# Block 2's attention with plain float32 products of 64 rows or columns, two heads at a time

## Chip, cores and metric

One core of a Trainium2 chip runs the whole program in one launch. The metric is the device time of the execution in microseconds. The engines are the tensor engine (PE, with its weight loads as PEld), the vector engine (DVE), the scalar engine (ACT), GpSimd (POOL) and the sync engine (SP), which issues the DMAs of the weights.

## The reference, cut

A first block (a mixer with pooling, attention and a recurrent branch, then a gated feed-forward layer), and after it a block of two layers, whose mixer has three kinds of attention with heads of 64 channels. Sequence 256, model width 2048, all float32.

```python
# layer l of block 2
h = rmsnorm_2(x, norm_mix[l])
qa, ka, va, qb, kb, vb, qc, kc, vc = jnp.split(h @ w_in[l], IN_SPLITS, axis=-1)
oa = window_attention(qa, ka, va, a_sink[l], t5_table)   # 8 heads, 2 of keys and values; bias, sink
ob = neighborhood_attention(qb, kb, vb, b_rpb[l])        # 8 heads; bias and a mask by column
oc = axial_global_attention(qc, kc, vc, c_q_gain[l], c_k_gain[l])  # 16 heads, 4 of keys; rms norm, rotary
# each: s = q k.T / 8 (+ bias); p = softmax(s); o = p v
mix = concat([rmsnorm_2(oa, ...), rmsnorm_2(ob, ...), rmsnorm_2(oc, ...)])
x = x + mix @ w_o[l]
u = relu(rmsnorm_2(x, norm_mlp[l]) @ w_up[l])
x = x + (u * u) @ w_down[l]
```

## The kernel before

Everything large is a product of activations (features on the partitions, 256 tokens in the free dimension) with a weight that is streamed from HBM in units of 128 x 1024 values. A unit is loaded by SP into one of 7 buffers, cut into a high and a low part of type float32r (line 136 on ACT, line 137 on DVE; 3 buffers each), and used in three float32r products per piece (lines 332 to 334, or 347 to 349 where the tokens are the output's partitions). `drive` writes the order by hand: the split of the next unit, then the products of this one, then one `step`.

The rest of the work runs beside the products as Python generators: each `step` advances every active generator by one stage and lets queues start new ones. The queue "rope" holds the norm and rotary part of C's keys and queries (lines 1459 to 1499, from line 1467 on ACT, a product with a block matrix on line 1470, and so on through DVE, ACT and POOL), the queue "head" the attention heads, one started per 1.4 steps. The order of instructions on each engine is that of the program; PE executes attention products between those of the units. Four PSUM banks ("a") are handed round among all generators, oldest first.

One head of block 2 (`head`, from line 1560) before the change: for each pair of heads `queries` (lines 1456 and 1457) makes [high; low] of one head's 64 query channels and [low; high] in 128 partitions; keys (`kk`) lie as high parts in both halves of the partitions and low parts in both, so that two products of 128 rows add all four combinations:

```python
nc.tensor.matmul(sc[:, i, :], qs[:, t], kh, start=True, stop=False)
nc.tensor.matmul(sc[:, i, :], qs[:, t], kl, start=False, stop=True)
```

This is done for two blocks of 128 queries: four float32r products. `softmax` (lines 1049 to 1067) takes the row maximum on DVE, the exponential on ACT, and scales; four transposes (line 1073) turn p; its high part is written on ACT (line 357), its low part on DVE (line 362); v has its high part in the first 64 output columns and its low part in the last 64, so four products (line 1620) give both halves, which line 1625 (ACT copies the lower half) and line 1626 (DVE adds it to the upper one) put together and write to `L["q"]`. Keys of A and C are split when they are made; B's keys for each pair of heads, in front of its scores. After the heads of a kind, `norm` (line 419 for the diagonal, 424 for the broadcast) prepares the rows for w_o.

Block 1's attention (`fox`) uses plain float32 products of full size, lines 1089, 1092 and 1108.

Of the kernel before, what the change touches and what calls it, by code (L numbers as in the profile page):

```python
# [9 lines left out]
F32 = mybir.dt.float32  # L10
F32R = mybir.dt.float32r
# [46 lines left out]
def shape_constants():  # L58
    """Arrays that follow from the shapes alone."""
# [59 lines left out]
class Unit:  # L119
    """A [128, nk, ncols] piece of a weight: loaded, cut into two float32r parts, used on the tensor engine."""  # L120
# [24 lines left out]
class Ada:  # L145
    """128 rows x 1024 columns of w_ada times silu(c), summed over the row tiles on the vector engine."""
# [44 lines left out]
def weave(a, b):  # L191
    """the two lists, evenly interleaved"""
# [7 lines left out]
class Builder:  # L200
# [51 lines left out]
    def bank(self):  # L252
        """the same for a PSUM bank"""
# [23 lines left out]
    def more_groups(self):  # L277
        """two of the banks go over to the column groups"""
# [3 lines left out]
    def fewer_groups(self):  # L282
        """the column groups leave them again; put back once what is in them has been read"""
# [37 lines left out]
    def mm_b(self, u, ps, X, first, last, k0=None, ncols=None):  # L321
        """PSUM[nb] += W[:, nb].T X for the rows of one unit; X = (hi, lo), features on the partitions."""
# [13 lines left out]
    def mm_a(self, u, outs, X, first, last, c0, n, shared=False):  # L336
        """outs[half] += X[:, half].T W for the rows of one unit: tokens on the partitions."""
# [13 lines left out]
    def split_to(self, hi, lo, src, scale=1.0):  # L351
        """hi + lo = src * scale, both float32r."""
# [36 lines left out]
    def sumsq_add(self, acc, src, first, scale=1.0):  # L389
        """acc (+)= (src * scale)^2"""  # L390
# [8 lines left out]
    def tok_sums(self, ps, *tiles):  # L399
        """Sum over the partitions of tiles of [128, n x 256] -> PSUM [128 tokens, 2]."""  # L400
# [9 lines left out]
    def rstd_of(self, r, ss, n):  # L410
        """r = (ss / n + eps) ** -0.5 of [128, 2]"""
# [9 lines left out]
    def bcast(self, ps, r, dg):  # L421
        """r [128 tokens, 2] -> PSUM [128, 256], each token's value in all partitions."""
# [1513 lines left out]
```

## Time and profile before

| | us |
|---|---|
| time, median of 3 runs | 3420.06 |
| lowest and highest | 3419.43 and 3421.57 |
| span of the profiled execution (its own time is not given apart) | 3419.7 |
| PE busy, PEld busy | 3282.7, 3231.9 |
| DVE busy, ACT busy, POOL busy | 2213.9, 1629.8, 294.4 |

Times in the profile are counted from the start of the span. Matmuls are pipelined: the record of one lasts longer than the distance to the next, so sums over records are more than the engine's time, and distances between starts are to be used. A plain float32 matmul leaves two records.

### The profile page before, as it was taken

The page shows a single profiled execution, that of the slowest core. Times are in us where ns is not written, and L with a number is a line of the kernel's source. Part 1 is how long each engine was busy: PE and PEld are TensorE (multiplying, and loading weights), DVE is VectorE, ACT ScalarE, POOL GpSimd, SP SyncE. Part 2 cuts the span into 40 slices and gives each one's busy share as a digit, 9 for nine tenths or more (in the row PEclk, how much of TensorE's full clock was granted, in tenths as well). Part 3 has the DMA queues.
Part 4 walks back from the last instruction along what each step waited for, and adds up shares of the span by engine and source line. Part 5 has one row for each costly group of instructions (what it writes and reads, how often), then busy time and mean ns, then how long its engine had stood idle before and what let it go on. Part 6 is the DMA issues. An engine that isn't in the chain of part 4 may idle for free.

```text
span 3419.7 us, 64015 instructions
## 1 busy us (share of the span) xinstructions
PE 3282.7 (96%) x26612; PEld 3231.9 (95%) x26612; DVE 2213.9 (65%) x2921; ACT 1629.8 (48%) x2236; POOL 294.4 (9%) x250
## 2 busy tenths in 40 slices
PE   7989899979999998999999999999999999999998
PEld 7988889979999998989999999998889999999998
DVE  7898887537745668976545454556897655545454
ACT  4436345424434456865434343445775533334344
POOL 0021100000000032111000000012110100000000
PEclk9999999999999999999999999999999999999999
DMA  9986896659866554545666665665454656666563
GB/s 360 336 286 224 300 318 225 187 169 304 273 200 187 184 160 122 162 143 180 185 185 185 185 186 183 186 182 154 133 161 153 182 184 185 185 185 185 183 186 125
DMA packets 390722, 683.96 MB, mean 200 GB/s; under 512 B 40823, under 2 KB 97952, under 8 KB 390176
## 3 DMA queue, kind: packets, MB, share of 16 engines
q1 hardware_dynamic: 390144, 679.56, 62.8%
q8 instruction: 208, 3.41, 0.4%
q14 instruction: 82, 0.67, 0.1%
q10 hardware_dynamic: 288, 0.31, 0.0%
HBM read 677.62 MB, written 8.46 MB: 201 GB/s over the span
## 4 chain that ended last, share of the span: by engine, by line
PE 77%; DVE 6%; DMA 2%; issue 2%; ACT 2%; SPq 1%; POOL 0%; ACTq 0%; DVEq 0%; POOLq 0%
PE pg L334 24%; PE pg L332 24%; PE pg L333 24%; DVE wlo L137 2%; ACT whi L136 1%; DMA raw<-in_w_ffn_up 1%; DMA raw<-in_w_ffn_gate 1%; DMA raw<-in_w_out 1%; PE pa L1620 1%; PE pa L1073 1%; DVE qs L1457 1%; DVE kB L362 0%; PE pa L1556 0%; DVE pr L1049 0%; DVE ada L171 0%
## 5 line engine op out<-in xcount | busy, mean ns | idle before, releaser
L137 DVE TENSOR_TENSOR wlo<-raw,whi 128x1024 fp32r<-128x1024 f32 x1064 | 1319.0, 1241 | 1089.0 <-ACT whi L136 1084.9
L136 ACT ACTIVATE whi<-raw 128x1024 fp32r<-128x1024 f32 x1064 | 1123.4, 1058 | 1554.0 <-PE pg L333 1254.1
L332 PE MATMUL pg<-xh,whi 128*128 128x256 f32 x5184 | 1478.6, 285 | 24.6 <-ACT whi L136 20.0
L334 PE MATMUL pg<-xh,wlo 128*128 128x256 f32 x5184 | 1468.2, 283 | 16.3 <-DVE wlo L137 16.2
L333 PE MATMUL pg<-xl,whi 128*128 128x256 f32 x5184 | 1467.0, 283 | 1.8 <-DVE xl L565 1.1
L332 PEld LDWEIGHTS pg<-xh,whi 128*128 128x128 f32 x5184 | 988.3, 191 | 30.4 <-ACT whi L136 21.2
L334 PEld LDWEIGHTS pg<-xh,wlo 128*128 128x128 f32 x5184 | 987.0, 190 | 20.8 <-DVE wlo L137 20.4
L333 PEld LDWEIGHTS pg<-xl,whi 128*128 128x128 f32 x5184 | 987.7, 191 | 6.9 <-issue 2.7
L332 PE MATMUL pg<-u,whi 128*128 128x256 f32 x2048 | 579.9, 283 | 0.0
L333 PE MATMUL pg<-u,whi 128*128 128x256 f32 x2048 | 579.5, 283 | 0.0
L334 PE MATMUL pg<-u,wlo 128*128 128x256 f32 x2048 | 579.5, 283 | 0.0
L333 PEld LDWEIGHTS pg<-u,whi 128*128 128x128 f32 x2048 | 393.1, 192 | 0.0
L334 PEld LDWEIGHTS pg<-u,wlo 128*128 128x128 f32 x2048 | 393.1, 192 | 0.0
L332 PEld LDWEIGHTS pg<-u,whi 128*128 128x128 f32 x2048 | 393.1, 192 | 0.0
L171 DVE SCALAR_TENSOR_TENSOR ada<-raw,cact,ada 128x1024 f32<-128x1024 f32 x180 | 234.8, 1304 | 19.1 <-DMA raw<-in_w_ada 18.1
L397 POOL TENSOR_TENSOR acc<-acc,t 128x512 f32<-128x512 f32 (+1 forms) x73 | 97.1, 1345 | 1372.3 <-ACT t L396 1361.0
L334 PE MATMUL pg<-uh,wlo 128*128 128x256 f32 x704 | 199.3, 283 | 0.0
L332 PE MATMUL pg<-uh,whi 128*128 128x256 f32 x704 | 199.3, 283 | 0.0
L333 PE MATMUL pg<-ul,whi 128*128 128x256 f32 x704 | 199.2, 283 | 0.0
L1820 POOL TENSOR_TENSOR y<-y 128x1024 f32<-128x1024 f32 x32 | 61.6, 1927 | 1200.0 <-ACT u L1819 1200.0
L332 PEld LDWEIGHTS pg<-uh,whi 128*128 128x128 f32 x704 | 135.1, 192 | 0.9 <-issue 0.9
L334 PEld LDWEIGHTS pg<-uh,wlo 128*128 128x128 f32 x704 | 135.1, 192 | 0.2 <-DVE wlo L137 0.2
(323 smaller groups left out, 2815.8 us busy)
## 6 DMA issues: line engine op xcount, KB each, us to landing
raw<-in_w_up SPq DMA_DIRECT2D x256, 512.0 KB
raw<-in_w_down SPq DMA_DIRECT2D x256, 512.0 KB
raw<-in_w_ada SPq DMA_DIRECT2D x192, 512.0 KB
raw<-in_w_in SPq DMA_DIRECT2D x192, 512.0 KB
raw<-in_w_ffn_gate SPq DMA_DIRECT2D x88, 512.0 KB
raw<-in_w_ffn_up SPq DMA_DIRECT2D x88, 512.0 KB
raw<-in_w_ffn_down SPq DMA_DIRECT2D x88, 512.0 KB
raw<-in_w_o SPq DMA_DIRECT2D x64, 512.0 KB
```

The source lines that it names most:

```text
L136: b.nc.scalar.activation(hi[:, :n], self.raw[:, :n], AF.Copy)
L137: b.nc.vector.tensor_tensor(lo[:, :n], self.raw[:, :n], hi[:, :n].bitcast(F32), ALU.subtract)
L171: b.nc.vector.scalar_tensor_tensor(g["acc"], self.raw, cs, g["acc"], ALU.mult, ALU.add)
L332: mm(o, wh, xh[:, k0 + j, :], start=st, stop=False, skip_group_check=True)
L333: mm(o, wh, xl[:, k0 + j, :], start=False, stop=False, skip_group_check=True)
L334: mm(o, wl, xh[:, k0 + j, :], start=False, stop=last and j == u.nk - 1, skip_group_check=True)
L397: nc.gpsimd.tensor_tensor(acc, acc, t, ALU.add)
L1073: self.nc.tensor.transpose(ps[:, k * S + i * P : k * S + (i + 1) * P], pr[:, i, k * P : (k + 1) * P], self.ident)
L1457: nc.vector.tensor_tensor(qs[b, h, :], raw[a], qs[a, h, :].bitcast(F32), ALU.subtract)
L1620: nc.tensor.matmul(o, v()[:, k].rearrange("p a d -> p (a d)"), pt[1][:, c, k, :], start=n == 0, stop=n == 3)
L1820: nc.gpsimd.tensor_tensor(flat(y), flat(y), flat(y), ALU.mult)
```

## The change

The two heads of a pair become one generator, `heads2`, started once per 2.8 steps. Queries, keys, v and p stay as they are in float32: no high and low parts. One head's 64 query channels lie in the lower, the other's in the upper half of the partitions, and the score products use 64 rows of the array each, with a bank for each head; p times v uses 64 columns for each head and writes the two halves of the partitions of one bank. Keys of a head that lie in the other half are copied there once (`other`, ACT). p's copy out of PSUM and the output's copy are on ACT alone; v is copied once. For C the two idle stages ahead of the scores go. There are 4 buffers for biases in place of 3, 6 for scores in place of 5, 4 for the turned p in place of 3. Comments were taken out as well; those lines are left out here, and the inner lines of long removed parts, which stand above.

```diff
@@ -1410,8 +1410,7 @@
...
-                qs=deque(range(2)), kB=deque(range(2)), bias=deque(range(3)), pr=deque(range(5)), pt=deque(range(3)),
-                y=deque(range(2)), rope=deque(range(1)),
+                bias=deque(range(4)), pr=deque(range(6)), pt=deque(range(4)), y=deque(range(2)), rope=deque(range(1)),
@@ -1422,14 +1421,17 @@
...
-            L["kA"] = ph.tile([P, 2, 2, S], F32R, name="kA")
-            L["kC"] = ph.tile([P, 2, 4, S], F32R, name="kC")
-            L["vA"] = ph.tile([P, 2, 2, 2, 64], F32R, name="vA")
-            L["vB"] = ph.tile([P, 2, 8, 2, 64], F32R, name="vB")
-            L["vC"] = ph.tile([P, 2, 4, 2, 64], F32R, name="vC")
+            L["ka"] = ph.tile([P, 2, S], F32, name="ka")
+            L["kc"] = ph.tile([P, 2, S], F32, name="kc")
+            L["kA"] = ph.tile([P, 2, S], F32, name="kA")
+            L["kC"] = ph.tile([P, 4, S], F32, name="kC")
+            L["vA"] = ph.tile([P, 2, 2, 64], F32, name="vA")
+            L["vB"] = ph.tile([P, 2, 8, 64], F32, name="vB")
+            L["vC"] = ph.tile([P, 2, 4, 64], F32, name="vC")
@@ -1443,26 +1445,26 @@
...
-        def kk(dst, c, raw):
...
-                nc.vector.tensor_tensor(qs[b, h, :], raw[a], qs[a, h, :].bitcast(F32), ALU.subtract)
+        def half(a):
+            return slice(a * 64, a * 64 + 64)
+        def other(dst, j, src):
+            nc.scalar.activation(dst[half(1 - j % 2), j, :], src[half(j % 2), j // 2, :], AF.Copy)
+        def keys_of(kind, g, a):
+            if kind == "b":
+                return L["kb"][half(a), g, :]
+            return L["k" + kind][half(a), g // 2, :] if g % 2 == a else L["k" + kind.upper()][half(a), g, :]
...
-            t0, t1 = (self.pt_(f"kB{n}", [P, 2, 512]) for n in (0, 1))
+            t0, t1 = (self.pt_(f"rope{n}", [P, 2, 512]) for n in (0, 1))
@@ -1493,16 +1495,15 @@
...
-                    kk(L["kC"], j, t[(j % 2) * 64 : (j % 2) * 64 + 64, j // 2, :])
-                    if j % 2 == 1:
-                        yield
+                    other(L["kC"], j, t)
+                yield
...
-            k = L["kb"][:, 0:2, :]
+            k = L["kc"]
@@ -1517,19 +1518,16 @@
...
-            raw = L["kb"][:, 2:4, :]
+            raw = L["ka"]
...
-                kk(L["kA"], j, raw[j * 64 : (j + 1) * 64, 0, :])
-                yield
+                other(L["kA"], j, raw)
...
-            for th in range(2):
-                v = b[1][:, th * P : (th + 1) * P].rearrange("p (h d) -> p h d", h=2)
-                self.split_to(L["vA"][:, th, :, 0, :], L["vA"][:, th, :, 1, :], v)
+            nc.scalar.activation(L["vA"].rearrange("p a b c -> p (a b c)"), b[1][:, :S], AF.Copy)
@@ -1547,85 +1545,80 @@
...
+            self.flags.add(f"kb{l}")
...
-        def stacked(sc, qs, kh, kl):
+        def heads2(t, kind, g, table, sink, near, need, values, last):
+            while not all(f"{f}{l}" in self.flags for f in need):
+                yield
+            bias = [None, None]
+            if table is not None:
+                for a in range(2):
+                    bias[a] = yield from self.take("bias", [P, 2, S])
+                    nc.sync.dma_start(bias[a][1], table(a).rearrange("(b p) k -> p b k", p=P))
+                yield
+                yield
+            if near:
+                for a in range(2):
+                    n = flat(bias[a][1]).rearrange("p (a c) -> p a c", c=64)
+                    nc.gpsimd.tensor_tensor(n, n, L["near"].unsqueeze(1).to_broadcast([P, 8, 64]), ALU.add)
+            pr = []
+            for a in range(2):
+                pr.append((yield from self.take("pr", [P, 2, S])))
+            while len(self.slots["a"]) < 2:
+                yield
+            bs = [self.bank_now() for _ in range(2)]
+            sc = [b[1].rearrange("p (a k) -> p a k", a=2) for b in bs]
...
-                t = slice(i * P, (i + 1) * P)
...
-            self.put("a", b)
+                for a in range(2):
+                    nc.tensor.matmul(
+                        sc[a][:, i, :], row(t)[half(a), i * P : (i + 1) * P], keys_of(kind, g[a], a), start=True, stop=True
+                    )
+            yield
+            soft = [
+                self.softmax(bs[a], sc[a], pr[a][1], bias[a][1] if bias[a] else None, sink(a) if sink else None, bias[a])
+                for a in range(2)
+            ]
+            while soft:
+                soft = [s for s in soft if next(s, DONE) is not DONE]
+                if soft:
+                    yield
+            yield
+            pt = []
+            for a in range(2):
+                pt.append((yield from self.take("pt", [P, 2, S])))
+                b = yield from self.bank()
+                self.transpose_p(b[1], pr[a][1])
+                self.put("pr", pr[a])
+                if a == 0:
+                    b0 = b
+            yield
+            for a, bb in enumerate((b0, b)):
+                nc.scalar.activation(flat(pt[a][1]), bb[1], AF.Copy)
+                self.put("a", bb)
...
-            n = 0
+            v = L["v" + kind.upper()]
...
-                for c in range(2):
...
-            nc.vector.tensor_tensor(row(t)[(h % 2) * 64 : (h % 2) * 64 + 64, :], o[:64, :], w[:64, :], ALU.add)
+                for a in range(2):
+                    vh = 2 * g[a] + a if kind == "b" else g[a]
+                    nc.tensor.matmul(
+                        o[half(a)], v[:, k, vh, :], pt[a][1][:, k, :], start=k == 0, stop=k == 1, skip_group_check=True
+                    )
+            for a in range(2):
+                self.put("pt", pt[a])
+            yield
+            nc.scalar.activation(row(t), o, AF.Copy)
...
-            if h % 4 == 3:
+            if t % 2 == 1:
@@ -1674,8 +1667,7 @@
...
-                    self.hi_of(L[name][:, th, :, 0, :], raw, r)
-                    self.lo_of(L[name][:, th, :, 1, :], L[name][:, th, :, 0, :], raw, r)
+                    nc.scalar.activation(L[name][:, th], raw, AF.Copy, scale=r)
@@ -1691,37 +1683,34 @@
...
-            self.rate("head", AHRATE)
+            self.rate("head", 2 * AHRATE)
...
-            for h in range(16):
-                g = h // 4
+            for i in range(8):
...
-                    head(16 + h, lambda g=g: (L["kC"][:, 0, g, :], L["kC"][:, 1, g, :]), lambda g=g: L["vC"][:, :, g],
-                         None, None, False, None, ("kc",), f"vc{l}", nn if h == 15 else None),
-                    f"qc{h // 4}.{l}",
+                    heads2(8 + i, "c", (i // 2, i // 2), None, None, False, ("kc",), f"vc{l}", nn if i == 7 else None),
+                    f"qc{i // 2}.{l}",
...
-            for h in range(8):
-                g = h // 4
+            for i in range(4):
...
-                    head(h, lambda g=g: (L["kA"][:, 0, g, :], L["kA"][:, 1, g, :]), lambda g=g: L["vA"][:, :, g],
-                         lambda h=h: self.bias_a[h], lambda h=h: L["sink"][:, h : h + 1], False, None, ("kva",), f"kva{l}",
-                         na if h == 7 else None),
+                    heads2(i, "a", (i // 2, i // 2), lambda a, i=i: self.bias_a[2 * i + a],
+                           lambda a, i=i: L["sink"][:, 2 * i + a : 2 * i + a + 1], False, ("kva",), f"kva{l}",
+                           na if i == 3 else None),
...
-            for h in range(8):
+            for i in range(4):
...
-                    head(8 + h, None, lambda h=h: L["vB"][:, :, h], lambda h=h: self.bias_b[l][h], None, True, h // 2,
-                         (), f"vb{l}", nb if h == 7 else None),
-                    f"qb{h // 4}.{l}",
+                    heads2(4 + i, "b", (i, i), lambda a, i=i: self.bias_b[l][2 * i + a], None, True,
+                           ("kb",), f"vb{l}", nb if i == 3 else None),
+                    f"qb{i // 2}.{l}",
```

## Rows read from the trace of the kernel before

**Rows 1.** The page, busy time of each engine with its share and instructions.

```profile
PE 3282.7 (96%) x26612; PEld 3231.9 (95%) x26612; DVE 2213.9 (65%) x2921; ACT 1629.8 (48%) x2236; POOL 294.4 (9%) x250
```

**Rows 2.** Stretches: length, busy us (count) of five engines, PE clock, DMA share, GB/s.

```profile
1240.00:1500.00 260.00, 231.88 (x1723) 219.85 (x1722) 223.06 (x498) 181.97 (x389) 51.70 (x41) 0.95 0.46 139
1360.00:1440.00 80.00, 79.56 (x670) 79.05 (x669) 73.38 (x188) 67.82 (x160) 5.86 (x3) 1.00 0.56 168
1440.00:1500.00 60.00, 50.77 (x299) 44.89 (x299) 53.94 (x130) 44.00 (x102) 13.53 (x11) 0.91 0.40 125
2340.00:2600.00 260.00, 235.76 (x1775) 224.13 (x1774) 226.57 (x489) 186.48 (x397) 48.30 (x34) 0.96 0.47 142
2520.00:2600.00 80.00, 69.79 (x450) 63.19 (x449) 71.50 (x161) 57.06 (x126) 13.87 (x11) 0.94 0.41 127
```

**Rows 3.** PE's weight loads, who waited for whom: us in total, times, longest.

```profile
PEld pa L1470 <- ACT kB L1467: 18.5, 6, 4.7
PEld pa L1556 <- DVE q L1626: 11.9, 6, 3.1
...
PEld pa L424 <- issue: 8.8, 2, 4.4
...
PEld pa L1073 <- DVE q L1626: 5.5, 4, 2.1
...
PEld pa L1620 <- DVE pt L362: 2.9, 2, 1.5
```

**Rows 4.** Instruction groups of DVE, 1235 to 1520 us: busy, mean ns, idle before.

```profile
L137 DVE TENSOR_TENSOR wlo<-raw,whi 128x1024 fp32r<-128x1024 f32 x67 | 85.8, 1281 | 31.2 <-ACT whi L136 30.6
L362 DVE TENSOR_TENSOR pt<-pa,pt 128x512 fp32r<-128x512 f32 x32 | 21.8, 683 | 0.3
L1457 DVE TENSOR_TENSOR qs<-q,qs 64x256 fp32r<-64x256 f32 x32 | 18.9, 591 | 4.2 <-ACT qs L1456 3.3
L1626 DVE TENSOR_TENSOR q<-pa,t 64x256 f32<-64x256 f32 x31 | 12.8, 414 | 0.5
...
L362 DVE TENSOR_TENSOR kB<-kb,kB 64x256 fp32r<-64x256 f32 x16 | 6.7, 420 | 0.5
```

**Rows 5.** The same view of ACT.

```profile
L357 ACT ACTIVATE pt<-pa 128x512 fp32r<-128x512 f32 x32 | 19.0, 594 | 5.6 <-PE pa L1073 5.1
...
L1456 ACT ACTIVATE qs<-q 64x256 fp32r<-64x256 f32 x32 | 13.1, 410 | 0.4
L1625 ACT ACTIVATE t<-pa 64x256 f32<-64x256 f32 x31 | 11.7, 378 | 0.6
```

**Rows 6.** PE in time (start, length), two heads of block 1, plain float32.

```profile
298.88 1.89 PE L1108 MATMUL pa<-pt,zv 128*128 128x256 f32 x8
300.60 0.60 PE L1073 MATMUL pa<-ident,pr 128*128 128x128 f32 x4
```

**Rows 7.** The same, two places in block 2, layer 0.

```profile
1393.83 0.64 PE L1620 MATMUL pa<-pt,vC 128*128 128x256 f32 x4
1394.31 0.28 PE L332 MATMUL pg<-xh,whi 128*128 128x256 f32 x1
...
1397.97 0.36 PE L1556 MATMUL pa<-kA,qs 128*128 128x256 f32 x1
...
1398.53 0.28 PE L332 MATMUL pg<-xh,whi 128*128 128x256 f32 x1
```

**Rows 8.** The same, the plain product with 33 rows.

```profile
635.60 0.28 PE L334 MATMUL pg<-uh,wlo 128*128 128x256 f32 x1
635.81 1.02 PE L1368 MATMUL pa<-oh,tb 33*8 33x511 f32 x2
636.76 0.39 PE L332 MATMUL pg<-uh,whi 128*128 128x256 f32 x1
```

**Rows 9.** The same, into products with 8 columns.

```profile
207.00 0.28 PE L334 MATMUL pg<-xh,wlo 128*128 128x256 f32 x1
207.12 0.28 PE L758 MATMUL pa<-xh,wfh 128*8 128x256 f32 x1
```

More of the change, by code (lines that the diff above doesn't have):

```diff
@@ L1444, in row @@
             return L["q"][t // 4][:, t % 4, :]
-        def kk(dst, c, raw):
-            for h in range(2):
-                o = slice(h * 64, (h + 1) * 64)
-                self.split_to(dst[o, 0, c, :], dst[o, 1, c, :], raw)
-        def queries(qs, raw):
-            for h in range(2):
-                a, b = slice(h * 64, (h + 1) * 64), slice((1 - h) * 64, (2 - h) * 64)
-                nc.scalar.activation(qs[a, h, :], raw[a], AF.Copy)
-                nc.vector.tensor_tensor(qs[b, h, :], raw[a], qs[a, h, :].bitcast(F32), ALU.subtract)
+        def half(a):
[6 more added lines that the diff above has]
+            return L["k" + kind][half(a), g // 2, :] if g % 2 == a else L["k" + kind.upper()][half(a), g, :]
         def rope(t, gain, done):
@@ L1549, in ev_kb @@
                 nc.vector.tensor_tensor(L["kb"][:, 2 * i : 2 * i + 2, :], ps[i], self.rb2(), ALU.mult)
+            self.flags.add(f"kb{l}")
             return
             yield
-        def stacked(sc, qs, kh, kl):
-            for i in range(2):
-                t = slice(i * P, (i + 1) * P)
-                nc.tensor.matmul(sc[:, i, :], qs[:, t], kh, start=True, stop=False)
-                nc.tensor.matmul(sc[:, i, :], qs[:, t], kl, start=False, stop=True)
-        def head(h, keys, v, table, sink, near, kpair, need, values, last):
+        def heads2(t, kind, g, table, sink, near, need, values, last):
@@ L1561, in head @@
             while not all(f"{f}{l}" in self.flags for f in need):
                 yield
-            t, pair = h // 2, (h // 2, "qs")
-            bias = None
+            bias = [None, None]
             if table is not None:
-                bias = yield from self.take("bias", [P, 2, S])
-                nc.sync.dma_start(bias[1], table().rearrange("(b p) k -> p b k", p=P))
-            if h % 2 == 0:
-                qs = yield from self.take("qs", [P, 2, S], F32R)
-                queries(qs[1], row(t))
-                L["qs", t] = qs
-                if kpair is not None:
-                    while f"qc3.{l}" not in self.flags:
-                        yield
-                    kB = yield from self.take("kB", [P, 2, 2, S], F32R)
-                    for j in range(2):
-                        kk(kB[1], j, L["kb"][j * 64 : (j + 1) * 64, kpair, :])
-                    L["kB", t] = kB
-                L[pair] = True
@@ L1580, in head @@
-            while pair not in L:
-                yield
-            qs = L["qs", t]
-            if kpair is not None:
-                kh, kl = L["kB", t][1][:, 0, h % 2, :], L["kB", t][1][:, 1, h % 2, :]
-            else:
-                kh, kl = keys()
-            yield
-            yield
-            if near:
-                n = flat(bias[1]).rearrange("p (a c) -> p a c", c=64)
-                nc.gpsimd.tensor_tensor(n, n, L["near"].unsqueeze(1).to_broadcast([P, 8, 64]), ALU.add)
-            pr = yield from self.take("pr", [P, 2, S])
@@ L1593, in head @@
-            b = yield from self.bank()
-            sc = b[1].rearrange("p (a k) -> p a k", a=2)
-            stacked(sc, qs[1][:, h % 2, :], kh, kl)
-            if h % 2 == 1:
-                self.put("qs", qs)
-                if kpair is not None:
-                    self.put("kB", L["kB", t])
-            yield
-            yield from self.softmax(b, sc, pr[1], bias[1] if bias else None, sink() if sink else None, bias)
-            yield
-            pt = yield from self.take("pt", [P, 2, 2, S], F32R)
@@ L1604, in head @@
-            b = yield from self.bank()
-            self.transpose_p(b[1], pr[1])
-            self.put("pr", pr)
-            yield
-            self.hi_of(flat(pt[1][:, 0]), b[1])
-            self.lo_of(flat(pt[1][:, 1]), flat(pt[1][:, 0]), b[1])
-            self.put("a", b)
+                for a in range(2):
+                    bias[a] = yield from self.take("bias", [P, 2, S])
+                    nc.sync.dma_start(bias[a][1], table(a).rearrange("(b p) k -> p b k", p=P))
+                yield
@@ new lines, in heads2 @@
+            sc = [b[1].rearrange("p (a k) -> p a k", a=2) for b in bs]
+            for i in range(2):
+                for a in range(2):
+                    nc.tensor.matmul(
+                        sc[a][:, i, :], row(t)[half(a), i * P : (i + 1) * P], keys_of(kind, g[a], a), start=True, stop=True
+                    )
+            yield
+            soft = [
+                self.softmax(bs[a], sc[a], pr[a][1], bias[a][1] if bias[a] else None, sink(a) if sink else None, bias[a])
+                for a in range(2)
+            ]
```

5 lines of the change are left out of this document (removed).

## Prediction

> **What bounds the kernel now.** I read the busy line of the page first: the tensor engine (PE) is busy for 3282.7 of 3419.7 us [rows 1], so the time is PE's work plus the stretches in which PE waits or runs at a lower clock. The table of stretches tells where the change can act. The attention of layer 0 of block 2 runs at 1240 to 1500 us, woven into the products with w_in_2 and w_o_2, that of layer 1 at 2340 to 2600 us [rows 2]. In these 2 x 260 us PE is idle for 28.1 and 24.2 us (260 minus its busy time). The granted clock has means of 0.95 and 0.96 there, so some of the time PE ran at the lower of its two levels (1.2 in place of 2.4 GHz): 0.05 x 260 + 0.04 x 260 = 23.4 us of work. So at most 52.3 + 23.4 = 75.7 us can be won by taking waits away. In the middle, 1360 to 1440, PE is full (79.56 of 80) at full clock, and there any matmul time added is added to the span [rows 2].
>
> Then the waits of PE's weight loads, because the order of instructions on PE is fixed and a late operand shows there. Block 2's attention has these: 11.9 us where scores wait for a PSUM bank that the last addition of an earlier head (line 1626, on DVE) still reads, 5.5 us where transposes wait for the same, 2.9 us where p times v waits for the low part of p, 8.8 us at the broadcast of a norm, and 18.5 us where the norm of the rotary part waits for ScalarE (ACT) [rows 3]. The 8.8 us are called "issue" in that view; the broadcast's diagonal is made on DVE, which is behind with its queue. The first four, 29.1 us, lead to DVE, which is busy for 223 and 227 of 260 us [rows 2]. DVE works in order, and its splits of the weights (85.8 us for layer 0, [rows 4]) stand in one queue with the attention's pieces.
>
> **What the change removes.** Per layer DVE loses the low parts of p (21.8 us), the splits of the queries (18.9), the additions of the two output halves (12.8) and the splits of B's keys (6.7) [rows 4], 60 us together, and some smaller ones of C's and A's keys and of v. DVE falls from some 223 to about 160 us of 260. ACT loses the high parts of the queries (13.1) and about half of the copies of outputs (11.7 for the 31 of 64 rows shown, for which 16 of 128 rows come); the copies of p stay (19.0) [rows 5]. With 160 of 260 us DVE would be filled to 62%, less than PE, and ACT by some 17 us less than before: neither limits a step of the weave any more, and ACT's copy of p, now the only work between transposes and p times v, keeps its 0.6 us a head [rows 5].
>
> What of PE's waits goes with that? The 29.1 us above stand behind additions and low parts that no longer exist, or behind DVE's backlog of key and query splits, and I take all of them. PE's clock is down mostly behind those stalls: 0.91 over the 60 us from 1440, 0.94 over the 80 us from 2520 [rows 2], 5.4 + 4.8 = 10.2 us. Of the 18.5 us at the rotary norm I take 5.5: its chain goes through ACT, POOL and DVE one after the other and stays, but splits of C's keys and of the first queries stand in DVE's queue in the middle of it. Sum: 29.1 + 10.2 + 5.5 = 45 us less. The bounds are 75.7 less (all loss gone) and 11 more: scores now read the rotated queries themselves, in the step in which these are announced, with no split and no two idle steps between; eight times (four groups of C's queries in each layer) at 1.4 us, a stall like that for one low part (2.9 us in 2 times [rows 3]), would be 11. Behind such scores the next unit's products stand in PE's queue, and behind those ACT's next weight part, which waits for its buffer. What is late next is that, and the rotary chain. POOL's addition to B's bias and the bias DMAs on SP keep their number; SP waits less for a bias buffer, there being four.
>
> **What it adds to PE.** Before, a head has four products for its scores and four for p times v, each one float32r record, and these take 0.48 us (1393.83 to 1394.31) and 0.56 us (1397.97 to 1398.53) [rows 7]. Two heads: 2 x 1.04 = 2.08 us. After, two heads have four plain float32 products for scores and four for p times v. What a plain product of 256 columns costs is seen in block 1: four of them (8 records, so two each) start at 298.88 and the next work starts at 300.60 [rows 6], 0.215 us a record, 0.43 a product. A pair of heads has 8 products, 16 records.
>
> How much of that runs side by side no row of before shows, since no two matmuls there use different halves of the array. The bounds: one after the other, 16 x 0.215 = 3.44 us; fully side by side, half, 1.72 us. Between them lies what the order of issue gives if a half may start as soon as its predecessors have started: a head's second record waits for its first, the other head's first starts with it, and so on; 8 records then take 5 record times, not 8 or 4. That is 5/8 of 3.44 = 2.15 us. I take this value: the operands are in different partitions (scores) or go to different ones (p times v), and the scores of the two heads have a bank each, so I see no shared cell or bank, only the order.
>
> Going into and out of a half costs something too. The one product of before with few rows (33) starts 0.21 us after the matmul before it, where 0.12 is usual; at the end, its two records of 511 columns (0.43 each by the price above) would be over at 636.67, and the next starts at 636.76, with its weights loaded only then [rows 8]. So 0.09 + 0.09, 0.2 us for a group of scores. Products with few columns show no such gap: 0.12 us from one to the next [rows 9]; for p times v I take 0. A pair then costs 2.15 + 0.2 = 2.35 us, 0.27 more than before. There are 16 pairs in each of 2 layers: 32 x 0.27 = 9 us more. By the bounds: 32 x (3.64 - 2.08) = 50 more, or 32 x (1.92 - 2.08) = 5 less.
>
> The Trainium skill, on the page "TensorE: Matmul & The Clock Gate", Part 3, says that matmuls in different row or column groups run at the same time and start some 4 ns apart. No run here shows it yet; by it alone the pair would be at the lower bound, and the sum 14 us lower.
>
> The transposes of p stay (8 of a pair), and so does what is around.
>
> **Sum.** Against the profiled execution, whose span is 3419.7 us (the page gives no other time for it; the median of the runs, 3420.06, is 0.4 above): 3419.7 - 45 + 9 = 3384 us.
>
> **Rivals.** (1) The halves run one after the other, and each change of half shows its weight load as the 33-row product does. Then the pair costs 3.64 us and six more changes at 0.1: 32 x (1.56 + 0.6) = 69 more on PE, and 3419.7 - 45 + 69 = 3444. Slower from the point where overlap saves less than 0.75 us of a pair (69 - 45 = 24, by 32). For it: no overlap of two products is shown, and the 33-row product delayed the load behind it. Against it: with few columns nothing is delayed [rows 9].
> (2) Entering and leaving halves costs a drain at all four borders of a pair. A matmul lasts 0.28 us where the next starts after 0.12 [rows 9], so a drain shows 0.16, in all 128 x 0.16 = 20 us in place of the 6 above: 3384 + 14 = 3398. Against it speak the 0.09 of rows 8 and the none of rows 9. The Trainium skill states such a rule: "TensorEngine Tiling (Array Packing)", Key Properties, has the tensor engine drained at each change of tiling mode.
> (3) Only one of the two kinds overlaps, or the waits move rather than go (to the rotary chain, or to ACT, which now frees the output's bank): 15 us less gained or 21 more on PE, around 3402 to 3412.
> (4) All overlaps, and most of the lost 75.7 us comes back: 3419.7 - 60 - 5 = 3355.
>
> **How the numbers follow.** Forecast 0.42, (1) 0.24, (2) 0.10, (3) 0.15, (4) 0.09. Around the forecast 3366 to 3402. A measurement here can tell 0.2% (6.8 us) from no change: 3413 to 3427. Faster: 0.42 + 0.10 + 0.09 and a part of (3), 0.65. The rest of (3) and the milder end of (1), where the loads are hidden (3419.7 - 45 + 50 = 3425), give the same, 0.13; the rest of (1) is slower, 0.22. The range, 3355 to 3436, leaves out the upper part of (1) and a part of (4).
>
> **What would show it.** Right: in the profile after, the waits for line 1626 and for the low part of p are gone, DVE is under 175 us busy in each attention, PE is idle for under 15 us there. The 8 records of a pair's scores go from the first start to the next work in about 1.1 us. If they take 1.7, rival (1) holds; if 1.1 with a hole of 0.16 or more at each border, rival (2). If DVE falls as said but PE's idle time stays, what is wrong is the step from DVE's load to PE's waits. The prediction is wrong if the time is above 3413, or if it is 3384 with other parts: no wait gone and less PE work.

## The result and the profile after

The changed kernel takes 3379.4 us (median of 4 runs, 3377.95 to 3380.27) against 3420.18 us (3419.43 to 3421.57) for the kernel before beside it. The ratio is 0.9881, with a 95% interval of 0.9867 to 0.9895: 41 us less, where 36 were forecast (3384). The profiled executions span 3378.5 and 3419.7 us, 41.2 us apart, and all accounts below are against this distance.

First the busy line of the page after; it answers to [rows 1].

```profile
PE 3279.3 (97%) x26612; PEld 3196.3 (95%) x26612; DVE 2096.3 (62%) x2661; ACT 1569.5 (46%) x2094; POOL 297.6 (9%) x250
```

PE executes as many instructions as before (16 float32r products of a pair have become 8 plain ones, of two records each) and is busy for 3.4 us less. DVE loses 118 us, ACT 60. With as many products on PE as before, the 41 us should lie in the time in which PE waited or ran at the lower clock. The table of stretches says where: the first two rows answer to the first and third of [rows 2], the last one is the attention of layer 1 at its new place. Columns are those of [rows 2].

```profile
1240.00:1500.00 260.00, 250.98 (x1901) 222.09 (x1900) 181.26 (x394) 164.97 (x338) 55.77 (x43) 0.99 0.51 152
...
1440.00:1500.00 60.00, 59.04 (x416) 49.76 (x415) 38.14 (x77) 37.68 (x74) 7.89 (x7) 1.00 0.51 157
2300.00:2560.00 260.00, 255.34 (x1949) 227.96 (x1948) 179.84 (x379) 166.68 (x340) 53.14 (x37) 0.99 0.52 155
```

A stretch of equal length holds more work after than before, because the work is done sooner. To compare the same work, each attention is taken here with the products around it, as long as it lasts in each kernel: first before, then after.

```profile
1236.00:1550.00 314.00, 285.88 (x2175) 273.64 (x2175) 259.40 (x550) 208.49 (x426) 57.48 (x46) 0.96 0.48 143
2310.00:2620.00 310.00, 285.76 (x2195) 274.08 (x2194) 254.00 (x522) 208.81 (x423) 54.55 (x39) 0.97 0.49 147
```

```profile
1236.00:1530.00 294.00, 284.98 (x2187) 255.98 (x2186) 202.35 (x422) 179.46 (x355) 60.43 (x46) 0.99 0.52 155
2290.00:2580.00 290.00, 285.34 (x2199) 257.85 (x2199) 195.85 (x397) 178.44 (x352) 55.66 (x39) 0.99 0.53 157
```

Each layer is 20 us shorter. PE's idle time (length minus busy) falls from 28.1 and 24.2 us to 9.0 and 4.7: 38.6 us of the 41.2. DVE has 57 and 58 us less. Outside these two stretches the run is as long as before, 2794.5 us after and 2795.7 before, so nothing was won there. PE is busy for as long as before in the two, 571.6 and 570.3 us together. That is a balance: the granted clock rose from 0.95 and 0.96 (over the 260 us of [rows 2]) to 0.99, which gives back 0.04 x 260 + 0.03 x 260 = 18 us, with a few us of doubt since the clock is given to 0.01 (added up in stretches of 20 us, the loss is 23 us before and 5 after); and the attention's own products became dearer, by some 17 us (below).

Now the waits of PE's weight loads over the whole run (who waited, for whom: us, times, longest), to be held against [rows 3]:

```profile
PEld pg L332 <- issue: 15.5, 42, 1.1
PEld pg L334 <- DVE wlo L137: 14.0, 17, 1.9
PEld pa L1472 <- ACT rope L1469: 10.2, 6, 3.5
...
PEld pa L424 <- DVE dg L419: 1.2, 3, 0.4
```

The waits for line 1626 and for the low part of p have no successor of their size. The broadcast of the norm waits 1.2 us in place of 8.8, the rotary norm 10.2 in place of 18.5. One row has grown: 42 short waits, 15.5 us, of line 332, the weight product that follows a group of half products; 40 of them lie in the two attention stretches. Before, it was

```profile
PEld pg L332 <- issue: 4.5, 10, 1.1
```

These waits are seen best in time (start, length), at a pair's p times v and a pair's scores in layer 0 after:

```profile
1378.57 0.27 PE L334 MATMUL pg<-xh,wlo 128*128 128x256 f32 x1
1378.77 1.08 PE L1613 MATMUL pa<-pt,vC 128*64 128x256 f32 x8
1379.79 0.39 PE L332 MATMUL pg<-xh,whi 128*128 128x256 f32 x1
1380.01 0.28 PE L333 MATMUL pg<-xl,whi 128*128 128x256 f32 x1
...
1382.61 0.27 PE L334 MATMUL pg<-xh,wlo 128*128 128x256 f32 x1
1382.81 0.48 PE L1578 MATMUL pa<-ka,q 64*128 64x256 f32 x1
1382.82 0.48 PE L1578 MATMUL pa<-kA,q 64*128 64x256 f32 x1
1383.13 0.38 PE L1578 MATMUL pa<-ka,q 64*128 64x256 f32 x1
1383.14 0.38 PE L1578 MATMUL pa<-kA,q 64*128 64x256 f32 x1
...
1383.56 0.38 PE L1578 MATMUL pa<-ka,q 64*128 64x256 f32 x1
1383.57 0.38 PE L1578 MATMUL pa<-kA,q 64*128 64x256 f32 x1
1383.88 0.39 PE L332 MATMUL pg<-xh,whi 128*128 128x256 f32 x1
1384.10 0.28 PE L333 MATMUL pg<-xl,whi 128*128 128x256 f32 x1
```

The two heads' scores (`ka` in the lower, `kA` in the upper half) start 0.01 us apart, four times: eight records in four record times. The group has seams at both ends: its first record starts 0.20 us after the unit's last, where 0.12 is usual, the second 0.32 after the first, where 0.21 is the rate, and the unit goes on 0.31 after the last. In all 1.07 us from first start to next work, where four records at 0.215 would be 0.86. p times v, in column halves, has nearly the same seams: 0.20 in, then 1.02. And the first weight product behind either group is followed by the next one after 0.22 us, where 0.12 is usual (1383.88 to 1384.10, 1379.79 to 1380.01).

The Trainium skill, "TensorE: Matmul & The Clock Gate", Part 3, says that matmuls in different row or column groups run at the same time. The trace agrees: 0.01 us between starts.

### The profile page after: what moved, and what is told of

The parts are those of the page before. It is cut to its first block, busy times and chain, and to the rows that moved or that the text cites. A ratio compares the mean times of both kernels' runs of the same rounds, so it can differ in the third digit from the quotient of the medians.

```text
span 3378.5 us, 63581 instructions
## 1 busy us (share of the span) xinstructions
PE 3279.3 (97%) x26612; PEld 3196.3 (95%) x26612; DVE 2096.3 (62%) x2661; ACT 1569.5 (46%) x2094; POOL 297.6 (9%) x250
## 4 chain that ended last, share of the span: by engine, by line
PE 80%; DVE 3%; DMA 3%; ACT 2%; issue 2%; SPq 0%; POOL 0%; ACTq 0%; DVEq 0%; POOLq 0%
PE pg L332 25%; PE pg L334 25%; PE pg L333 25%; DVE wlo L137 1%; DMA raw<-in_w_ffn_up 1%; PE pa L1578 1%; PE pa L1613 1%; PE pa L1073 1%; ACT whi L136 1%; DVE ada L171 1%; PE pg L347 1%; PE pg L348 1%; PE pg L349 1%; DMA raw<-in_w_ada 0%; DMA raw<-in_w_out 0%
## 5 line engine op out<-in xcount | busy, mean ns | idle before, releaser
L332 PE MATMUL pg<-xh,whi 128*128 128x256 f32 x5184 | 1479.1, 285 | 24.7 <-ACT whi L136 20.3
```

The lines of the kernel that those rows point to most:

```text
L332: mm(o, wh, xh[:, k0 + j, :], start=st, stop=False, skip_group_check=True)
```

## Experiments

The theory after the result: (a) most of the gain is DVE's relief, since PE's waits and lowered clock in the attention stood behind DVE's queue and behind banks that DVE released late; (b) it is kept only because the halves run side by side. Rivals: the gain is one of fewer waits for banks, whoever reads them; it is one of the deeper buffers and dropped idle steps; or the product side gained. The last is refuted by the stretches above: the products became dearer. Differences "from the kernel after" below are between medians of different groups of runs. The kernel before had medians of 3419.68 to 3422.49 in these groups, so some 3 us of such a difference are uncertain; ratios are to the kernel before in the same group.

**The order of issue.** My 5/8 rested on it.

```diff
-            for i in range(2):
-                for a in range(2):
+            for a in range(2):
+                for i in range(2):
                     nc.tensor.matmul(   # scores; the same swap of k and a in p times v
```

> The changed kernel with the two loops over block and head exchanged in both products: first the two products of one head, then those of the other. If each half of the array works through its own products, whatever stands between them in program order, a group of 8 records still takes 4 record times of 0.215 us, and the time stays at 3379 us (within 3). If products start in program order, only the last record of one head and the first of the other run side by side, a group takes 7 record times, 0.65 us more in each of 64 groups: 3379 + 41 = 3420 us.

Measured: 3378.99 us (3377.07 to 3379.32), ratio 0.9872 [0.9855, 0.9888], the same as after. In program order there are now four records of the lower half ahead of four of the upper one; on the chip (same view):

```profile
1292.15 0.48 PE L1578 MATMUL pa<-kc,q 64*128 64x256 f32 x1
1292.16 0.48 PE L1578 MATMUL pa<-kC,q 64*128 64x256 f32 x1
...
1293.22 0.39 PE L332 MATMUL pg<-xh,whi 128*128 128x256 f32 x1
```

The second head does not wait for the first one's products: the group takes 1.07 us from first start to next work, and the time lies on the first expectation, not on 3420. So the overlap is the same in both orders, and my step "the order of issue gives 5/8" is wrong. (The trace lists records by their start; that PE was handed them in the program's order is taken from the kernel and not seen in it.)

**Both heads' scores in the same half of rows.** The upper head's scores are left out (the lower head's are computed twice); instructions and records are as many.

```diff
-  sc[a][:, i, :], row(t)[half(a), i * P : (i + 1) * P], keys_of(kind, g[a], a), ...
+  sc[a][:, i, :], row(t)[half(0), i * P : (i + 1) * P], keys_of(kind, g[0], 0), ...
```

> The changed kernel with the score products of both heads taken from the lower half of the partitions (the upper head's own scores are left out of the computation). Theory, two halves run side by side and that is what makes the plain product affordable: a group of scores takes 8 instead of 4 record times of 0.215 us, 0.86 us more in 32 groups, 3379 + 27 = 3406 us. Rival, what a group costs is its start and its end and not its records: no change, 3379 us (within 4).

Measured: 3401.76 us (3401.1 to 3403.02), ratio 0.9941 [0.9926, 0.9955], 22 us more than after. One pair in time:

```profile
1292.58 0.27 PE L334 MATMUL pg<-xh,wlo 128*128 128x256 f32 x1
1292.78 1.99 PE L1578 MATMUL pa<-kc,q 64*128 64x256 f32 x8
1294.70 0.39 PE L332 MATMUL pg<-xh,whi 128*128 128x256 f32 x1
```

1.92 us in place of 1.07, 0.85 x 32 = 27 us of PE's time. The 22 measured are less; over the same work (1236 to 1541 and 2301 to 2602 us here) PE's idle time is 6.7 + 3.8 us, where it was 9.0 + 4.7, so 3 of the 27 filled time that PE had lost.

**Both heads' p times v in the same columns**, the kind that e2 did not test:

```diff
-  o[half(a)], v[:, k, vh, :], pt[a][1][:, k, :], start=k == 0, stop=k == 1, ...
+  b[1][half(0), a * S : a * S + S], v[:, k, vh, :], pt[a][1][:, k, :],
+  start=k == 0 and a == 0, stop=k == 1, ...
-            nc.scalar.activation(row(t), o, AF.Copy)
+            for a in range(2):
+                nc.scalar.activation(row(t)[half(a)], b[1][half(0), a * S : a * S + S], AF.Copy)
```

> The changed kernel with p times v of both heads on the lower 64 columns of the array: both outputs go to the lower half of the partitions, side by side in the bank, and ACT copies each to its place (two copies of 64x256 in place of one of 128x256, on ACT, which has room). Nothing of the computation is left out. Theory, column halves run side by side as the halves of rows do: a group takes 0.86 us more, 32 groups, of which, as in e2_same_half (27 reckoned, 23 seen), a little is hidden: 3400 to 3407 us. Rival, column halves never ran side by side: 3379 to 3383 us.

Measured: 3402.03 us (3399.06 to 3402.42), ratio 0.9938 [0.9921, 0.9955], 23 us more than after, as expected. A p times v with scores behind it:

```profile
1326.44 0.28 PE L334 MATMUL pg<-xh,wlo 128*128 128x256 f32 x1
1326.65 1.94 PE L1612 MATMUL pa<-pt,vC 128*64 128x256 f32 x8
1328.52 0.48 PE L1578 MATMUL pa<-kc,q 64*128 64x256 f32 x1
```

1.87 us in place of 1.02. Both kinds overlap fully, and each overlap is worth 22 to 23 us. If the two add up, the change without either would be at 3379.4 + 22.4 + 22.6 = 3424 us, no gain on 3420; both were not taken away in one kernel.

**DVE's load given back.** The kernel after, with as many DVE instructions per pair of heads as the splits of queries, p and B's keys and the additions were, writing to a tile in SBUF that nobody reads:

```diff
+            for a in range(2 if kind != "b" else 6):     # in front of the scores
+                nc.vector.tensor_tensor(dj[half(a % 2), :S], row(t)[half(a % 2)], row(t)[half(a % 2)], ALU.subtract)
...
+                nc.vector.tensor_tensor(dj, flat(pt[a][1]), flat(pt[a][1]), ALU.subtract)   # per head, behind p's copy
...
+            for a in range(2):                            # at the output
+                nc.vector.tensor_tensor(dj[half(a), :S], row(t)[half(a)], row(t)[half(a)], ALU.add)
```

> The changed kernel with DVE work of the kind and place that the change took away, on SBUF operands into a scrap tile that nobody reads: two of 64x256 ahead of a pair's scores (six for B), one of 128x512 for each head at p's copy, two of 64x256 at the output. DVE gets some 55 to 60 us a layer back, PE and ACT get nothing, and no PSUM bank is held longer. Theory, DVE's backlog made PE's waits: a good part of the 41 us comes back, 3395 to 3412 us. Rival, it was not the load but that banks were released by DVE (or that heads now come in pairs): 3379 to 3385 us.

Measured: 3408.63 us (3407.53 to 3412.08), ratio 0.9962 [0.9947, 0.9977], 29 us more than after. The stretches of equal length as after (columns of [rows 2]):

```profile
1236.00:1530.00 294.00, 273.71 (x2054) 244.28 (x2053) 242.95 (x520) 171.67 (x345) 61.57 (x46) 0.98 0.47 145
2290.00:2580.00 290.00, 276.45 (x2081) 248.66 (x2080) 242.05 (x496) 175.40 (x350) 57.36 (x39) 0.96 0.49 151
```

and the waits of PE's loads:

```profile
PEld pa L1472 <- ACT rope L1469: 16.0, 6, 3.6
...
PEld pa L1073 <- DVE s L414: 9.5, 2, 5.1
...
PEld pa L1581 <- DVE s L1049: 4.9, 3, 2.3
```

DVE is busy for some 83% of both stretches, as in the stretches of equal work before; PE is idle for 20.3 + 13.6 us, and the rotary norm waits nearly as long as in [rows 3]. Nothing that was added makes a value that is used: waits that name it are 0.8 us of PE and 7.5 us of POOL in the whole run. Over the same work (1236 to 1544 and 2304 to 2608 us here) PE is idle for 20 us more than after, and the clock's 0.98 and 0.97 in place of 0.99 make up the rest of the 29. So DVE's load alone takes back 29 of the 41 us. ACT, which lost 29 and 30 us over the same work, stays as light as after here; no run gives ACT its load back, so a share of ACT is not tested.

**The same load, reading the PSUM banks**, so that DVE also releases them:

```diff
-                nc.vector.tensor_tensor(dj, flat(pt[a][1]), flat(pt[a][1]), ALU.subtract)
+                nc.vector.tensor_tensor(dj, bb[1], flat(pt[a][1]), ALU.subtract)
...
-                nc.vector.tensor_tensor(dj[half(a), :S], row(t)[half(a)], row(t)[half(a)], ALU.add)
+                nc.vector.tensor_tensor(dj[half(a), :S], o[half(a)], row(t)[half(a)], ALU.add)
```

> As e3_dve_load (3408.6 us), but two of DVE's scrap operations read what they read before the change: the PSUM bank of the turned p, and that of the output, which are so held until DVE has come to them. Theory, the holding of banks by a late DVE is a cause of its own beside the load: 3415 to 3425 us, with waits of PE for these lines as before. Rival, the length of DVE's queue alone counts: 3405 to 3412 us.

Measured: 3412.09 us (3409.18 to 3413.14), ratio 0.9972 [0.9961, 0.9983], a tenth of a microsecond above the rival's range and below the theory's. The intervals of this kernel and the last one overlap: in the time no effect of the banks is shown beyond that of the load, and 3 us are the most likely size of one. In the waits the banks do show:

```profile
PEld pa L1073 <- DVE dj L1606: 9.4, 2, 4.7
```

Transposes wait for a bank that the added operation on p still reads. In return the rotary norm waits 10.2 us here and 16.0 in the kernel with the load alone, and PE's idle time in the two stretches is nearly the same (35.0 and 33.9 us). So the load moves the total, and which line waits differs from kernel to kernel.

**DVE's load taken from the kernel before.** The low part of p and the upper half of the output are left out; PE's products stay as many.

```diff
-            self.lo_of(flat(pt[1][:, 1]), flat(pt[1][:, 0]), b[1])
...
-  nc.tensor.matmul(o, v()[:, k].rearrange("p a d -> p (a d)"), pt[1][:, c, k, :], ...)
+  nc.tensor.matmul(o, v()[:, k].rearrange("p a d -> p (a d)"), pt[1][:, 0, k, :], ...)
...
-            w = self.tmp(S)
-            nc.scalar.activation(w[:64, :], o[64:128, :], AF.Copy)
-            nc.vector.tensor_tensor(row(t)[(h % 2) * 64 : (h % 2) * 64 + 64, :], o[:64, :], w[:64, :], ALU.add)
+            nc.scalar.activation(row(t)[(h % 2) * 64 : (h % 2) * 64 + 64, :], o[:64, :], AF.Copy)
```

> The kernel before, with the low part of p left out of the computation (p times v uses the high part twice, so PE does the same products) and with the output's upper half left out (one copy by ACT in place of copy and addition). DVE loses 34.6 of the 60 us a layer that the change takes from it, PE's work is the same, the output's bank is released by ACT. Theory, PE's waits of before came from DVE's backlog and from the banks that it held: 3385 to 3400 us, and the waits for lines 1626 and 362 are gone from PE. Rival, the gain comes from the pairing of heads and the shape of the products: 3415 to 3420 us.

Measured: 3401.27 us (3400.01 to 3401.75), ratio 0.9938 [0.9923, 0.9953]: 20 us less than before, just beside the theory's range and well below the rival's. Its waits, to be held against [rows 3]:

```profile
PEld pa L1470 <- ACT kB L1467: 17.0, 6, 4.7
...
PEld pa L424 <- issue: 8.0, 2, 4.0
...
PEld pa L1556 <- ACT q L1623: 4.0, 4, 1.8
```

What waited for the addition is down to 4.0 us (line 1623 is ACT's copy now). The rotary norm and the broadcast keep theirs; that these want more of DVE's relief than this kernel gives is my reading, and no run shows it.

**Only the output's addition taken away**, the part of the last one that frees a bank:

```diff
-            w = self.tmp(S)
-            nc.scalar.activation(w[:64, :], o[64:128, :], AF.Copy)
-            nc.vector.tensor_tensor(row(t)[(h % 2) * 64 : (h % 2) * 64 + 64, :], o[:64, :], w[:64, :], ALU.add)
+            nc.scalar.activation(row(t)[(h % 2) * 64 : (h % 2) * 64 + 64, :], o[:64, :], AF.Copy)
```

> The kernel before, with the output's upper half left out of the computation, so that ACT's copy frees the bank in place of DVE's addition (DVE loses 12.8 us a layer, ACT's work stays, p's low part stays on DVE). Of the 20 us that e5_before_light_dve won: if the bank's release by DVE is the cause, most of it is won here too, 3401 to 3408 us; if DVE's load is, a share of 12.8 in 34.6, some 7 us: 3411 to 3416 us.

Measured: 3407.94 us (3407.6 to 3411.05), ratio 0.9964 [0.995, 0.9978], 13.6 us less than before. That is two thirds of the 20, for 12.8 of the 34.6 us of DVE's work that e5 removes per layer [rows 4]. In the old form, with one head at a time, an addition that holds a bank until DVE's queue comes to it does cost more than its share of the load, by the first of the two expectations; in the new form (the two kernels with the load given back) the time does not show it. What is left waits for the low part of p:

```profile
PEld pa L1556 <- DVE pt L362: 4.4, 3, 1.5
...
PEld pa L1620 <- DVE pt L362: 2.9, 2, 1.5
```

**The buffers and idle steps of before.** The change also deepens three pools and drops two idle steps for C's heads, which I had priced at nothing but for a possible stall.

```diff
-  bias=deque(range(4)), pr=deque(range(6)), pt=deque(range(4)), ...
+  bias=deque(range(3)), pr=deque(range(5)), pt=deque(range(3)), ...
...
-                yield
-                yield
+            yield
+            yield
             if near:
```

> The changed kernel with the buffers of before (3 for biases, 5 for scores, 3 for the turned p) and with the two idle stages ahead of C's scores again. Theory, these parts of the change hide behind PE: 3377 to 3383 us. Rival, the shorter way of C's first heads is part of the gain: 3385 to 3390 us, with idle time of PE at the beginning of the attention.

Measured: 3409.6 us (3407.54 to 3410.4), ratio 0.9965 [0.9952, 0.9978]: 30 us more than after, outside both ranges. Two of PE's waits have grown, from 1.4 and 0.8 us after:

```profile
PEld pg L333 <- DVE xl L362: 9.8, 7, 3.0
...
PEld pg L332 <- ACT xh L357: 6.0, 3, 2.6
```

These are w_o's products waiting for the attention's rows: the heads end later than the products that should cover them. Two more kernels take the parts singly. Only the three pools:

> Only the buffers of e7_stages_of_before: 3 for biases, 5 for scores, 3 for the turned p, and no idle stages for C. Theory, the 30 us that e7 lost come from the buffers: a pair takes two of each, so with an odd number the next pair waits in the middle and all later heads with it: 3400 to 3410 us, with waits of PE for the rows of w_o's input. Rival, they come from C's two idle stages: 3377 to 3383 us.

Measured: 3392.96 us (3388.2 to 3393.9), ratio 0.9918 [0.9904, 0.9933], 13.6 us more than after, between the two expectations. Scores now wait for a bank that DVE's line 1049 still reads, up to 4.8 us at a time:

```profile
PEld pa L1578 <- DVE s L1049: 8.8, 2, 4.8
```

By the kernel's text a pair takes two buffers of each pool, so three or five serve no more pairs than two or four; which of the three pools it is was not tried. Only the two idle steps:

> Only the two idle stages ahead of C's scores of e7_stages_of_before, with the buffers of the changed kernel. By the theory of e9_buffers_of_before: 3377 to 3385 us. By its rival, C's later outputs keep PE waiting at w_o: 3400 to 3410 us. If both parts only hurt together, both runs stay near 3380 us.

Measured: 3383.68 us (3382.9 to 3385.48), ratio 0.9895 [0.988, 0.991], 4 us more than after, in the first of its ranges and with an interval that overlaps that of after. 13.6 and 4.3 make 18 of the 30; the other 12 come only with both, and the waits for w_o's rows are long only in that kernel (2.3 us for line 333 with the pools alone, 1.4 with the idle steps alone). That the two delays add up until the heads end too late fits this, but no run takes it apart.

**Two rotary buffers.** Apart from the seams, the largest wait that is left in the attention, 10.2 us, is at the rotary norm, whose tiles one unit at a time may use.

```diff
-  rope=deque(range(1)),
+  rope=deque(range(2)),
...
-            t0, t1 = (self.pt_(f"rope{n}", [P, 2, 512]) for n in (0, 1))
+            t0, t1 = (self.pt_(f"rope{lock[0]}{n}", [P, 2, 512]) for n in (0, 1))
```

> The changed kernel with two rotary generators at a time, each with its own scrap tiles, in place of one. 10.2 us of PE's remaining waits are at the product of the rotary norm, behind ACT, which waits to write the tiles that DVE still reads for the group before. Theory, that wait is one for the tiles: 4 to 10 us less, 3370 to 3375 us. Rival, ACT, POOL and DVE are simply late in that stretch, or the two chains get into each other's way: 3377 to 3385 us.

Measured: 3375.26 us (3372.23 to 3375.69), ratio 0.9863 [0.9849, 0.9878], between its two ranges. The wait is down to 1.3 us; small ones of the scores for the rotated queries came:

```profile
PEld pa L1578 <- DVE q L1493: 3.1, 3, 1.8
```

> The same kernel as e6_two_ropes (3375.3 us), for the interval. If its 4 us are no chance: 3371 to 3377 us; if they are, 3377 to 3381 us.

Measured again: 3376.19 us (3374.28 to 3377.56), ratio 0.987 [0.9854, 0.9887], in the first of its ranges. Both times 3 to 4 us under the kernel after, but the intervals of the ratios overlap with 0.9867 to 0.9895: likely better, not certain.

## Why the prediction was right

The time came where forecast, 4.6 us below it, and the mechanism named, DVE's queue behind PE's waits, is borne out. That it came so close is in part luck: the waits gave back 12 us more than forecast and the products took 8 more, and 30 us of the gain hang on the numbers of buffers and idle steps, which the sum did not weigh.

**Waits, -45 forecast.** By this account idle time and clock were to give 45 us. Idle time gave 38.6, the clock some 18, 57 together. The term was too small by 12, mostly in the clock, for which I had counted only the two stretches behind stalls (10.2). The waits of [rows 3] went as named: the banks and the low part of p fully, the broadcast from 8.8 to 1.2 us, the rotary norm by 8.3 where I took 5.5. I had not counted the wait for the low weight parts; this is its row of before:

```profile
PEld pg L334 <- DVE wlo L137: 21.8, 21, 2.1
```

Of these, 7.4 us lie in the two attention stretches, and none does after; the 14.0 us of after stand ahead of 1236 us, where nothing was changed.

That DVE's load is a cause is shown from both sides: giving it back costs 29 us (e3), taking 34.6 of the 60 us a layer from the kernel before wins 20 (e5). The bank that DVE holds is a part of it in the old form (e8). It is not the only condition: with the old pools and idle steps 30 of the 41 us are lost though DVE is as light as after (e7). The 29 and the 30 overlap and can't be added, and the kernel before was not run with deeper pools. "DVE under 175 us in each attention" failed by its letter (181 and 180 in 260 us), since these 260 us now hold more of the weights' work. DVE's fall over the same work is 57 and 58 us, where 60 was forecast; ACT's is 29 and 30, where some 17 were, since the high parts of the keys were left out of that sum. PE's idle time is under the 15 us named.

**Products, +9 forecast.** Measured some 17, from three wrong sizes, two of which nearly cancel. The pair before costs 1.88 us and not 2.08. The prediction names the two places of [rows 7] in reverse: the first is p times v, 0.48, the second scores, 0.56, and these stood behind transposes, the last of which starts only 0.03 us ahead of them. Other groups of the kernel before go on at the usual 0.12 from the first to the fourth product and out of the group:

```profile
1378.58 0.28 PE L1556 MATMUL pa<-kC,qs 128*128 128x256 f32 x1
...
1378.94 0.28 PE L1557 MATMUL pa<-kC,qs 128*128 128x256 f32 x1
1379.05 0.28 PE L332 MATMUL pg<-xh,whi 128*128 128x256 f32 x1
1379.17 0.28 PE L333 MATMUL pg<-xl,whi 128*128 128x256 f32 x1
```

Groups of either kind that have no wait and do not stand behind transposes take 0.47 us a head; those behind transposes start 0.09 earlier and take 0.56. After, the overlap is complete, 16 records in 8 record times, 1.72 in place of 2.15 us. And the seams cost 0.70 us a pair, not 0.2: the medians over groups without a wait are 1.06 for scores and 1.02 for p times v, 0.09 more at each entry, and behind each group the next product holds PE for 0.06 (a transpose) to 0.10 us longer than it did before, 0.16 a pair: 2.42 in all, less 1.72. So 2.42 - 1.88 = 0.54, times 32 = 17 us (a little less where a p times v stands right before scores). The step that failed here is the seam: I had taken p times v to have none because products with 8 columns have none [rows 9], and the halves of columns do. It is 16 us over the 32 pairs, and the full overlap gives 14 of them back.

**What was costed at nothing.** The stall of scores that read the rotated queries at once (up to 11 us) did not come: no such wait is in the list after. The opposite sign was missed. Dropping the idle steps and having even numbers of buffers are worth up to 30 us together (e7). I read "four bias buffers in place of three" only as fewer waits on SP, and did not ask how many buffers a pair takes. With the old numbers the same change ends at 3410, outside the 3366 to 3402 around the forecast.

**The rivals.** (1), one half after the other, is refuted by the trace of after, and e2 and e12 show what it would have cost: some 45 us if the two add up, more than the whole gain. (2) has its condition met in size: all four borders cost, 0.70 us together where it said 0.64 and I said 0.2. Its sum, 3398, took the overlap, the pair before and the waits from my forecast, and so did not come. The Trainium skill's rule, "TensorEngine Tiling (Array Packing)", Key Properties, that the engine drains at a change of tiling mode, agrees with these seams; it gives no price. (3) is refuted in both forms: both kinds overlap, and the waits did not move. (Its 15 and 21 us lead from 3384 to 3399 and 3405, not to 3402 to 3412.) (4) was right that all overlaps and that most of the loss comes back (57 of 75.7 us); its -5 for the products was the lower bound without seams, where +17 was measured.

**Against the sum:** -38.6 idle, -18 clock and +17 products make -40, where 41.2 were measured; the 1 to 2 us are within what the clock's 0.01 leaves open.

## What to carry to other kernels

Where one engine's waits stand behind another engine's queue, removing work from that queue shortens waits of instructions that never used this work: price it by all waits in the stretch and by the clock lost there, not only by the lines that name the removed instruction. Two small products that fit into different halves of the array cost about one, plus a seam of some 0.35 us per group, and were as fast in both orders of the program that were tried. When the unit of work doubles, look at each pool of buffers as a number of units, since an odd one is left over.

## What the chip showed that I had not expected

Products of different halves start beside each other in both orders of the program that were tried: with all of the lower half's ahead, the starts are still 1292.15 and 1292.16. A group pays its seams at both ends and in both kinds of halves: 0.20 us in place of 0.12 before the first record, 0.32 (0.27 in column halves) in place of 0.21 to the second, 0.31 in place of 0.21 behind the last, and 0.22 in place of 0.12 from the full product behind it to the next. And a p times v with scores right behind it saves only one entry and one such slow full product by that (kernel after, in time):

```profile
1328.69 0.28 PE L334 MATMUL pg<-xh,wlo 128*128 128x256 f32 x1
1328.90 1.08 PE L1613 MATMUL pa<-pt,vC 128*64 128x256 f32 x8
1329.91 0.48 PE L1578 MATMUL pa<-kc,q 64*128 64x256 f32 x1
...
1330.98 0.39 PE L332 MATMUL pg<-xh,whi 128*128 128x256 f32 x1
```

From 1328.90 to 1330.98 are 2.08 us for the 16 records, as 1.02 and 1.06 apart; the change from column to row halves costs what a change to full products does.
